# Hybrid GLA/SSD block on one core: the clamped difference of the SSD decay matrix on ScalarE instead of VectorE

## The chip, the cores and the metric

The kernel runs on one core of a Trainium2 chip. The metric is the device time of one execution in microseconds (us), lower is better; the median of three executions of the kernel before is 1922.84 us (1921.1 to 1924.56).

A core has five engines that run their own instruction streams in order: TensorE (PE in the profile, its weight loads PEld), VectorE (DVE), ScalarE (ACT), GpSimd (POOL) and SyncE (SP, which here only issues DMAs). They meet through semaphores.

## The reference, cut to what matters

One layer over 2048 tokens of width 1024, float32: RMS norm, an input projection, gated linear attention (GLA, 4 heads), a state space part (SSD, 16 heads of width 64 in 2 groups), an output projection, and a gated embedding part. The change lies in the SSD part. For each head the reference computes, chunk by chunk,

```python
cum = jnp.cumsum(dti * a_g, axis=1)
seg = cum[:, :, None] - cum[:, None, :]
decay_ij = jnp.where(causal, jnp.exp(jnp.minimum(seg, 0.0)), 0.0)
cb = jnp.einsum('bign,bjgn->bijg', ci, bi)
y = jnp.einsum('bijgh,bjghp->bighp', cb[..., None] * decay_ij, xdt)
y = y + jnp.einsum('bign,bghpn->bighp', ci, state) * jnp.exp(cum)[..., None]
```

So for each pair of tokens i, j of a chunk the decay is exp(min(cum_i - cum_j, 0)), and it multiplies the masked product cb.

## The kernel before, in words

The kernel takes the tokens in four blocks of 512 (the loop over b). Every large product is made of float32r matmuls in three parts (high by high, high by low, low by high): `prep_w` splits each weight tile with a copy on ScalarE (L172, `whi`) and a subtraction on VectorE (L173, `wlo`), and `dense_t` and `dense_n` issue the matmuls (L203 to L205, L222 to L226, in `out_proj` L794 to L796). The smaller work of GLA and SSD is written as Python generators (`gla_steps`, `ssd_steps` and others) in a list `side`; `step()` advances each by one piece between two dense products.

The order written in the file is not the order on an engine. The framework's scheduler places the instructions on each engine when the kernel is built, by priority in program order and by when it reckons an operand is ready; so independent pieces lie interleaved in the trace. On the chip each engine then keeps to that order.

In each block `ssd_steps` runs twice, once for each group g of 8 heads. It goes over four chunks t of 128 tokens:

- `make_x(t)`: transposes, `xd` on VectorE (L534), `xe` on GpSimd (L537), its split into `xh` on ScalarE (L541) and GpSimd (L542).
- `make_m(t)`: two tiles `em` (q = 0, 1) of [128, 4 heads, 128]. Partition j holds the row cum_i of four heads, read from DRAM to all partitions (L550, issued by SP). Four VectorE instructions, one for each head, subtract cum_j and clamp at zero (L552), ScalarE takes the exponential of the whole tile (L555), VectorE multiplies by `cb` (L556). The pool has three `em` tiles, so a DMA for the next waits until TensorE has read the oldest.
- the chunk: the old state times `ctl` into `ips` (L574), `em` times `xd` into `yps` (L579), the new state (L582 to L584), then on VectorE `S` (L587), `ec` (L588), `xs` (L590, L592). Then `make_x` and `make_m` of the next chunk.

`gla_steps` runs between these pieces: products into PSUM tile `ups` (from L451 on), a scaled copy `st` of the state `gT` on ScalarE (L485), the sum on VectorE (L486, `gT`), the product with `st` on TensorE (L488) and a square on ScalarE (L489). GLA and SSD share four PSUM buffers (`pss`), so a matmul that begins a new one waits until VectorE or ScalarE has read the oldest.

The change touches L552 and L555 inside `make_m`:

Of the kernel before, what the change touches and what calls it, by code (L numbers as in the profile page):

```python
# [10 lines left out]
AF = mybir.ActivationFunctionType  # L11
ALU = mybir.AluOpType
# [23 lines left out]
def hybrid_kernel(ctx, tc, x_nat, x_t, p_t, w_t, w_n0, w_n, w_o, w_g, w_p, prm, gup, cst, out):  # L36
    nc = tc.nc
    mm = nc.tensor.matmul
    act = nc.scalar.activation
# [58 lines left out]
    for h in range(GH):  # L98
        t = state.tile([P, 256], F32, name=f"gT{h}")
# [3 lines left out]
    for g in range(2):  # L103
        t = state.tile([P, 512], F32, name=f"sS{g}")
# [3 lines left out]
    for h in range(GH):  # L108
        t = sm.tile([P, NT + 1], F32, name="gD", tag=f"gD{h}", bufs=2)
# [400 lines left out]
    def ssd_steps(g, bt, ctl, xs, cx):  # L510
        h8 = slice(8 * g, 8 * g + 8)
        S = sS[g]
        S3 = S.rearrange("p (h c) -> p h c", c=64)
        dt, cum, elast, dte, cd, ecd = (cx[n] for n in ("dt", "cum", "elast", "dte", "cd", "ecd"))
        bps = pss.tile([P, TB], F32, name="pss")
        for t in range(NT):
            nc.tensor.transpose(out=bps[:, t * P:(t + 1) * P], in_=bt[:, t, :], identity=ident)
        bn = sb.tile([P, 2, NT, P], F32R, name="bn", tag="bn", bufs=SB["bn"])
        bp3 = bps.rearrange("p (a b) -> p a b", b=P)
        nc.scalar.copy(out=bn[:, 0], in_=bp3)  # L520
        tt(out=bn[:, 1], in0=bp3, in1=bn[:, 0].bitcast(F32), op=ALU.subtract)
        cps = pss.tile([P, TB], F32, name="pss")
        for t in range(NT):
            mm(out=cps[:, t * P:(t + 1) * P], lhsT=bt[:, t, :], rhs=ctl[:, t, :], start=True, stop=True)
        cb = sb.tile([P, NT, P], F32, name="cb", tag="cb", bufs=SB["cb"])
        tt(out=cb, in0=cps.rearrange("p (a b) -> p a b", b=P),
           in1=tri.unsqueeze(1).broadcast_to([P, NT, P]), op=ALU.mult)

        def make_x(t):
            xps = pss.tile([P, TB], F32, name="pss")  # L530
            for m in range(4):
                nc.tensor.transpose(out=xps[:, m * P:(m + 1) * P], in_=xs[:, m, t * P:(t + 1) * P], identity=ident)
            xd = sb.tile([P, 8, 64], F32, name="xd", tag="xd", bufs=SB["xd"])
            tt(out=xd, in0=xps.rearrange("p (h c) -> p h c", c=64),  # L534
               in1=dt[:, t, h8].unsqueeze(2).broadcast_to([P, 8, 64]), op=ALU.mult)
            xe = sb.tile([P, 8, 64], F32, name="xe", tag="tmp", bufs=SB["tmp"])
            nc.gpsimd.tensor_tensor(out=xe, in0=xd, in1=dte[:, t, h8].unsqueeze(2).broadcast_to([P, 8, 64]),  # L537
                                    op=ALU.mult)
            xh = sb.tile([P, 2, 512], F32R, name="xh", tag="xh", bufs=SB["xh"])
            xef = xe.rearrange("p h c -> p (h c)")  # L540
            nc.scalar.copy(out=xh[:, 0, :], in_=xef)  # L541
            nc.gpsimd.tensor_tensor(out=xh[:, 1, :], in0=xef, in1=xh[:, 0, :].bitcast(F32), op=ALU.subtract)  # L542
            return xd, xh

        def make_m(t):
            ems = []
            for q in range(2):
                em = sb.tile([P, 4, P], F32, name="em", tag="em", bufs=SB["em"])
                h4 = 8 * g + 4 * q
                nc.sync.dma_start(out=em, in_=cd[t, h4:h4 + 4, :].partition_broadcast(P))  # L550
                for hh in range(4):
                    nc.vector.tensor_scalar(out=em[:, hh, :], in0=em[:, hh, :],  # L552
                                            scalar1=cum[:, t, h4 + hh:h4 + hh + 1], scalar2=0.0,
                                            op0=ALU.subtract, op1=ALU.min)
                act(out=em, in_=em, func=AF.Exp)  # L555
                tt(out=em, in0=em, in1=cb[:, t, :].unsqueeze(1).broadcast_to([P, 4, P]), op=ALU.mult)  # L556
                ems.append(em)
            ec = sb.tile([P, 4, P], F32, name="ec", tag="ec", bufs=SB["ec"])
            for hf in range(2):
                src = ecd[t].rearrange("(m two) i -> two m i", two=2)[hf, 4 * g:4 * g + 4, :]  # L560
                nc.sync.dma_start(out=ec[64 * hf:64 * hf + 64], in_=src.partition_broadcast(64))
            return ems, ec

        yield
        nx = make_x(0)
        nm = make_m(0)
        yield
        for t in range(NT):
            ts = slice(t * P, (t + 1) * P)
            xd, xh = nx  # L570
            ems, ec = nm
            ips = pss.tile([P, TB], F32, name="pss")
            for m in range(4):
                mm(out=ips[:, m * P:(m + 1) * P], lhsT=S[:, m * P:(m + 1) * P], rhs=ctl[:, t, :],  # L574
                   start=True, stop=True)
            yps = pss.tile([P, TB], F32, name="pss")
            for m in range(4):
                for z in range(2):
                    mm(out=yps[64 * z:64 * z + 64, m * P:(m + 1) * P], lhsT=xd[:, 2 * m + z, :],  # L579
                       rhs=ems[m // 2][:, 2 * (m % 2) + z, :], start=True, stop=True)  # L580
            nps = pss.tile([P, TB], F32, name="pss")
            mm(out=nps, lhsT=bn[:, 0, t, :], rhs=xh[:, 0, :], start=True, stop=False)  # L582
            mm(out=nps, lhsT=bn[:, 0, t, :], rhs=xh[:, 1, :], start=False, stop=False)
            mm(out=nps, lhsT=bn[:, 1, t, :], rhs=xh[:, 0, :], start=False, stop=True)  # L584
            nc.gpsimd.tensor_tensor(out=S3, in0=S3, in1=elast[:, t, h8].unsqueeze(2).broadcast_to([P, 8, 64]),
                                    op=ALU.mult)
            tt(out=S, in0=S, in1=nps, op=ALU.add)  # L587
            tt(out=ec, in0=ec, in1=ips.rearrange("p (m i) -> p m i", i=P), op=ALU.mult)  # L588
            for m in range(4):
                stt(out=xs[:, m, ts], in0=xs[:, m, ts], scalar=pr[:, C_D + 4 * g + m:C_D + 4 * g + m + 1],  # L590
                    in1=yps[:, m * P:(m + 1) * P], op0=ALU.mult, op1=ALU.add)
            tt(out=xs[:, :, ts], in0=xs[:, :, ts], in1=ec, op=ALU.add)  # L592
            if t + 1 < NT:
                nx = make_x(t + 1)
                nm = make_m(t + 1)
                yield
# [74 lines left out]
    for b in range(NB):  # L671
# [135 lines left out]
        for t in range(NT):  # L807
            r = 1.0 if b else rn[:, t:t + 1]
            nc.vector.tensor_scalar_mul(out=lrn[:, t, :, 0:16],
                                        in0=outs[t][:, 256:272].unsqueeze(1).broadcast_to([P, 4, 16]), scalar1=r)  # L810
            stt(out=dtr[:, t, :], in0=outs[t][:, 272:288], scalar=r, in1=pr[:, C_DTB:C_DTB + 16],
                op0=ALU.mult, op1=ALU.add)
# [237 lines left out]
```

## Time and profile before

| | before |
|---|---|
| median of three executions | 1922.84 us |
| span of the profiled execution (first to last instruction) | 1915.8 us |
| TensorE busy | 1848.5 us, 96% |
| VectorE busy | 1402.0 us, 73% |
| ScalarE busy | 929.5 us, 49% |
| GpSimd busy | 372.3 us, 19% |
| DMA, mean | 108 GB/s |

The page gives the span as the profiled execution's own time; the medians are taken around the whole execution, and lie 7.0 us above it. TensorE is busy nearly throughout, so the time can fall only where TensorE stands idle or runs at a lower granted clock. Those places are found by stretches of time, not by the shares of the whole span.

### The profile page before, as it was taken

The numbers are of one execution on the slowest core, as the hardware profiler recorded it, in microseconds if no ns is written. First come the engines' busy times: TensorE is split into PE (matmuls) and PEld (weight loads), VectorE is DVE, ScalarE is ACT, GpSimd is POOL, SyncE is SP. The second block draws the span as 40 slices with busy tenths as digits, with TensorE's granted clock in tenths as the row PEclk, the third lists the DMA queues.
The fourth block names the chain that finished last, engine by engine and source line by source line (L and its number), as shares of the span: only waits on it lengthen the run. The fifth ranks groups of instructions, "written<-read, shape, count | busy, mean of one in ns | idle before, by whom it ended". The sixth has DMA issues, their size and how long they took to land.

```text
span 1915.8 us, 27885 instructions
## 1 busy us (share of the span) xinstructions
PE 1848.5 (96%) x10418; PEld 1577.9 (82%) x10418; DVE 1402.0 (73%) x2689; ACT 929.5 (49%) x1692; POOL 372.3 (19%) x331
## 2 busy tenths in 40 slices
PE   8989999999999999999999999999999999999997
PEld 7868888877887888877788788897778788889886
DVE  8996686587788668558678766855877877684676
ACT  6545443465554553346555355334655445533563
POOL 3022031043112103004311210300430211030122
PEclk9999999999999999999999999999999999999998
DMA  4332242233443233223344323322334432232232
GB/s 138 121 110 88 79 158 73 88 110 122 170 125 100 82 107 125 77 78 110 124 177 121 101 77 115 117 89 77 123 113 165 135 97 78 92 104 82 68 119 77
DMA packets 80888, 206.56 MB, mean 108 GB/s; under 512 B 8048, under 2 KB 26736, under 8 KB 80368
## 3 DMA queue, kind: packets, MB, share of 16 engines
q1 hardware_dynamic: 78768, 198.21, 32.5%
q0 software_dynamic: 1984, 6.55, 0.9%
q8 instruction: 82, 1.34, 0.3%
q14 instruction: 54, 0.44, 0.1%
HBM read 196.09 MB, written 8.65 MB: 107 GB/s over the span
## 4 chain that ended last, share of the span: by engine, by line
PE 70%; DVE 18%; ACT 5%; issue 3%; DMA 3%; POOL 1%; SPq 0%; DVEq 0%; ACTq 0%; POOLq 0%
PE psd L204 10%; PE psd L203 10%; PE psd L205 10%; PE psd L224 5%; PE psd L226 5%; PE psd L222 5%; PE psd L796 5%; PE psd L795 5%; PE psd L794 5%; DVE em L552 3%; DVE wlo L173 3%; PE pss L488 1%; DMA xp<-x_t 1%; DMA em<-cd 1%; DVE em L556 1%
## 5 line engine op out<-in xcount | busy, mean ns | idle before, releaser
L173 DVE TENSOR_TENSOR wlo<-wraw,whi 128x512 fp32r<-128x512 f32 (+1 forms) x560 | 423.9, 761 | 218.7 <-ACT whi L172 217.3
L172 ACT CAST whi<-wraw 128x512 fp32r<-128x512 f32 (+1 forms) x560 | 343.9, 620 | 466.0 <-PE psd L204 238.2
L205 PE MATMUL psd<-u,wlo 128*128 128x512 f32 x896 | 352.7, 394 | 2.1 <-DVE wlo L173 2.1
L203 PE MATMUL psd<-u,whi 128*128 128x512 f32 x896 | 353.7, 395 | 0.0
L204 PE MATMUL psd<-u,whi 128*128 128x512 f32 x896 | 351.8, 393 | 0.9 <-POOL u L331 0.9
L222 PE MATMUL psd<-whi,u 128*128 128x256 f32 (+1 forms) x960 | 276.5, 288 | 0.0
L224 PE MATMUL psd<-wlo,u 128*128 128x256 f32 (+1 forms) x960 | 273.1, 284 | 2.1 <-DVE wlo L173 2.1
L226 PE MATMUL psd<-whi,u 128*128 128x256 f32 (+1 forms) x960 | 272.6, 284 | 0.0
L300 POOL TENSOR_TENSOR sq<-sq,sqt 128x512 f32<-128x512 f32 (+1 forms) x85 | 109.9, 1293 | 610.1 <-ACT sqt L297 610.1
L794 PE MATMUL psd<-mq,whi 128*128 128x512 f32 x512 | 205.4, 402 | 0.0
L796 PE MATMUL psd<-mq,wlo 128*128 128x512 f32 x512 | 202.1, 395 | 0.0
L795 PE MATMUL psd<-mq,whi 128*128 128x512 f32 x512 | 201.0, 393 | 0.0
L205 PEld LDWEIGHTS psd<-u,wlo 128*128 128x128 f32 x896 | 168.5, 188 | 39.4 <-DVE wlo L173 3.9
L204 PEld LDWEIGHTS psd<-u,whi 128*128 128x128 f32 x896 | 168.6, 188 | 34.1 <-POOL u L331 1.2
L203 PEld LDWEIGHTS psd<-u,whi 128*128 128x128 f32 x896 | 168.6, 188 | 33.5 <-ACT whi L172 0.6
L224 PEld LDWEIGHTS psd<-wlo,u 128*128 128x128 f32 x960 | 183.6, 191 | 5.3 <-DVE wlo L173 2.9
L222 PEld LDWEIGHTS psd<-whi,u 128*128 128x128 f32 x960 | 183.6, 191 | 2.4 <-ACT whi L172 1.0
L226 PEld LDWEIGHTS psd<-whi,u 128*128 128x128 f32 x960 | 183.6, 191 | 0.0
L797 DVE TENSOR_TENSOR ht<-ht,psd 128x512 f32<-128x512 f32 x128 | 86.9, 682 | 66.2 <-PE psd L796 65.9
L796 PEld LDWEIGHTS psd<-mq,wlo 128*128 128x128 f32 x512 | 96.3, 188 | 20.6 <-issue 0.7
L203 PE MATMUL psd<-mq,whi 128*128 128x512 f32 (+1 forms) x288 | 107.3, 373 | 5.8 <-ACT pp L941 5.8
L795 PEld LDWEIGHTS psd<-mq,whi 128*128 128x128 f32 x512 | 96.4, 188 | 20.0 <-DVE mq L505 1.1
(248 smaller groups left out, 3274.0 us busy)
## 6 DMA issues: line engine op xcount, KB each, us to landing
wraw<-w_t SPq DMA_DIRECT2D x112, 512.0 KB, 3.5
wraw<-w_o SPq DMA_DIRECT2D x64, 512.0 KB, 3.5
wraw<-w_n SPq DMA_DIRECT2D x56, 512.0 KB, 3.5
em<-cd SPq DMA_DIRECT2D x64, 256.0 KB, 3.9
wraw<-w_g SPq DMA_DIRECT2D x32, 512.0 KB, 3.6
ec<-ecd SPq DMA_DIRECT2D x64, 128.0 KB, 3.0
xn<-x_nat SPq DMA_DIRECT2D x24, 256.0 KB, 3.4
xp<-x_t SPq DMA_DIRECT2D x24, 256.0 KB, 3.8
```

The lines of the kernel that those rows point to most:

```text
L172: nc.scalar.copy(out=hi, in_=s)
L173: tt(out=lo, in0=s, in1=hi.bitcast(F32), op=ALU.subtract)
L203: mm(out=ps, lhsT=hi[:, sl], rhs=rhi(k), start=(k == 0), stop=False)
L204: mm(out=ps, lhsT=hi[:, sl], rhs=rlo(k), start=False, stop=False)
L205: mm(out=ps, lhsT=lo[:, sl], rhs=rhi(k), start=False, stop=(k == KT - 1))
L222: mm(out=outs[t], lhsT=ug(0, k)[:, ts], rhs=hi[:, sl], start=first, stop=False, skip_group_check=True)
L224: mm(out=outs[t], lhsT=ug(0, k)[:, ts], rhs=lo[:, sl], start=False, stop=False, skip_group_check=True)
L226: mm(out=outs[t], lhsT=ug(1, k)[:, ts], rhs=hi[:, sl], start=False, stop=last, skip_group_check=True)
L300: self.eng.tensor_tensor(out=self.acc[:, cs], in0=self.acc[:, cs], in1=sq, op=ALU.add)
L794: mm(out=ps, lhsT=hi[:, sl], rhs=mq[:, 0, k, :], start=(k == 0), stop=False)
L795: mm(out=ps, lhsT=hi[:, sl], rhs=mq[:, 1, k, :], start=False, stop=False)
L796: mm(out=ps, lhsT=lo[:, sl], rhs=mq[:, 0, k, :], start=False, stop=(k == 3))
```

## The change

Four VectorE instructions `min(em - cum, 0)` become four ScalarE instructions `Relu(-em + cum)`, with `cum` as a bias per partition. Their result has the opposite sign, and the exponential gets the scale -1. The data, tiles, DMAs and matmuls are the same.

```diff
                 for hh in range(4):
-                    nc.vector.tensor_scalar(out=em[:, hh, :], in0=em[:, hh, :],
-                                            scalar1=cum[:, t, h4 + hh:h4 + hh + 1], scalar2=0.0,
-                                            op0=ALU.subtract, op1=ALU.min)
-                act(out=em, in_=em, func=AF.Exp)
+                    act(out=em[:, hh, :], in_=em[:, hh, :], func=AF.Relu, scale=-1.0,
+                        bias=cum[:, t, h4 + hh:h4 + hh + 1])
+                act(out=em, in_=em, func=AF.Exp, scale=-1.0)
                 tt(out=em, in0=em, in1=cb[:, t, :].unsqueeze(1).broadcast_to([P, 4, P]), op=ALU.mult)
```

## Rows read from the trace of the kernel before

**Rows 1.** The page's first part: busy time, share of the span, instructions.
```profile
PE 1848.5 (96%) x10418; PEld 1577.9 (82%) x10418; DVE 1402.0 (73%) x2689; ACT 929.5 (49%) x1692; POOL 372.3 (19%) x331
```

**Rows 2.** Windows: stretches with SSD work; length, busy time by engine, clock, DMA.
```profile
60.00:130.00 70.00, 63.73 (x368) 51.62 (x368) 65.56 (x138) 34.99 (x68) 17.14 (x15) 1.00 0.37 111
520.00:610.00 90.00, 85.62 (x507) 71.48 (x506) 77.72 (x178) 42.25 (x81) 16.71 (x15) 0.98 0.40 129
1000.00:1085.00 85.00, 80.60 (x470) 66.83 (x469) 71.53 (x161) 38.34 (x74) 16.72 (x15) 0.96 0.40 113
1480.00:1555.00 75.00, 70.70 (x403) 57.53 (x402) 66.96 (x150) 31.51 (x63) 16.93 (x15) 0.98 0.40 119
...
700.00:780.00 80.00, 76.04 (x482) 66.26 (x481) 66.80 (x131) 35.12 (x72) 19.39 (x21) 0.98 0.39 126
...
sum 610.00, PE 581.13 PEld 491.84 DVE 528.26 ACT 273.62 POOL 143.19; mean PE 72.64 PEld 61.48 DVE 66.03 ACT 34.20 POOL 17.90
```

**Rows 3.** Waits of TensorE: us in total, times, longest us.
```profile
PE pss L451 <- DVE gT L486: 15.4, 8, 2.1
PE pss L459 <- DVE ec L588: 5.5, 5, 1.6
PE pss L451 <- DVE ec L588: 2.2, 2, 2.0
```

**Rows 4.** The chain that ended last, 580 to 597: start us, us, what.
```profile
580.48 3.40 DVE em L552 x4
583.88 0.34 DVE gT L486
584.27 0.39 PE pss L451
...
594.06 2.61 DVE em L552 x4
596.67 0.34 DVE gT L486
```

**Rows 5.** Timeline of GpSimd beside the first four of those.
```profile
579.96 1.42 POOL L537 TENSOR_TENSOR xe<-xd,dte 128x512 f32<-128x512 f32 x1 [3.46 <-DVE xd L534]
581.34 1.04 POOL L585 TENSOR_TENSOR sS<-sS,elast 128x512 f32<-128x512 f32 x1
```

**Rows 6.** Line L552: min/median/max ns, and what VectorE waited for before it.
```profile
L552 DVE TENSOR_SCALAR em<-em,cum x256: 264/279/1528, 88.4 to 1713.0; 128x128 f32<-128x128 f32 x128
...
  DMA em<-cd: 5.5, 8
```

**Rows 7.** Windows just behind the first of those waits (columns as in rows 2).
```profile
585.00:590.00 5.00, 5.00 (x21) 3.31 (x21) 2.50 (x7) 1.81 (x5) 0.00 (x0) 0.66 0.14 41
```

**Rows 8.** Groups by line and shape: busy us, mean ns | idle before, releaser.
```profile
L552 DVE TENSOR_SCALAR em<-em,cum 128x128 f32<-128x128 f32 x256 | 106.7, 475 | 5.7 <-DMA em<-cd 5.5
...
L555 ACT ACTIVATE em<-em 128x512 f32<-128x512 f32 x64 | 40.4, 631 | 60.6 <-DVE em L552 60.5
L485 ACT ACTIVATE st<-gT,fs 128x256 f32<-128x256 f32 x64 | 31.9, 505 | 10.8 <-DVE gT L486 10.6
L425 ACT ACT_TABLE_LOAD x8 | 10.3, 1283 | 0.1
L950 ACT ACTIVATE gth<-gth 128x256 f32<-128x256 f32 x8 | 3.3, 418 | 7.0 <-DVE gth L949 7.0
L377 ACT ACTIVATE wk<-wk 128x64 f32<-128x64 f32 x4 | 1.0, 247 | 0.0
```

**Rows 9.** Timeline of ScalarE: two independent instructions, one behind the other.
```profile
542.06 0.62 ACT L446 ACTIVATE qm<-bc 128x512 f32<-128x512 f32 x1
542.58 0.62 ACT L447 ACTIVATE km<-bc 128x512 f32<-128x512 f32 x1
```

**Rows 10.** Timeline of VectorE, then of TensorE: a decay tile done, and its first use.
```profile
584.58 0.69 DVE L556 TENSOR_TENSOR em<-em,cb 128x512 f32<-128x512 f32 x1
...
585.51 0.43 PE L579 MATMUL pss<-em,xd 128*64 128x128 f32 x2
```

**Rows 11.** Waits of ScalarE: us in total, times, longest us.
```profile
ACT xh L541 <- POOL xe L537: 96.0, 32, 6.2
```

## The prediction, made before the changed kernel was run

> **What bounds the kernel now.** I read the page's busy shares first: TensorE is at 96% of the span [rows 1], so whatever the change does for VectorE, it pays only where TensorE stands still or is slowed. Next I cut the span into stretches around the eight places where the SSD chunks run (four blocks, two groups each) and read them as windows [rows 2]. Together they last 610.0 us, and TensorE is busy for 581.1 of them: 28.9 us idle, of the 67.3 us (1915.8 - 1848.5) that it idles in the whole span. The four stretches of group 0 hold 6.3, 4.4, 4.4 and 4.3 us of it, together 19.4; group 1 the other 9.5. VectorE is busy 528.3 us of the 610.0 there, 87%, against 73% overall; ScalarE only 273.6, 45%. So locally VectorE is the crowded engine, beside a TensorE with few holes.
>
> What ends the holes is seen in the list of waits [rows 3]: 15.4 us are waits of a GLA product (L451) for the sum `gT` on VectorE, eight times nearly 2 us, which is twice in each block; 7.7 us are waits for `ec` (L588), also VectorE. Why VectorE is late there is seen in the chain that ended last [rows 4]: in front of each late `gT` stand exactly four of the subtractions that the change takes away, 3.40 us in one place and 2.61 us in the other. These four should take 4 x 0.279 = 1.1 us by the median of the line, but its slowest took 1.528 us [rows 6], and they are slow while GpSimd works on `xe` and `sS` [rows 5]. Over the kernel the 256 subtractions cost VectorE 106.7 us, 475 ns in the mean [rows 8], so about a third of that is time lost beside GpSimd.
>
> The windows show one more loss: right behind a hole the granted clock of TensorE falls, to a mean of 0.66 over 5 us [rows 7], that is, part of that time at 1.2 instead of 2.4 GHz. From the stretches whose clock is under 1.00 [rows 2]: 90 x 0.02 + 85 x 0.04 + 75 x 0.02 + 80 x 0.02 = 8.3 us. All that there is to win in the eight stretches is then 28.9 + 8.3 = 37.2 us, 1.9%.
>
> **The change part by part.** *Removed:* 256 VectorE instructions, 106.7 us busy [rows 8]. Most of it is covered by TensorE and is worth nothing; what counts is the part in front of TensorE's holes. (a) The `gT` waits, 15.4 us: the four subtractions in front last longer (3.40 and 2.61) than the holes (about 1.9), so `gT` itself is no longer late. Next late is the decay tile, which was finished at 585.27 for a product at 585.51 [rows 10]. I count three quarters, 11.6 us (bounds 0 and 15.4). (b) The other idle time of these stretches, 28.9 - 15.4 = 13.5 us, mostly behind `ec`, which stands in VectorE's queue behind the same subtractions but also behind work that stays: half, 6.7 us (bounds 0 and 13.5). (c) The clock: it fell behind the holes, and I take half of the 8.3 back, 4.2 us (bounds 0 and 8.3). Sum of the gains 22.5 us.
>
> *Added:* 256 ScalarE instructions of 128x128 with a bias per partition. The trace has no such instruction. Nearest are one of 128x64 without a pointer operand, 247 ns, below, and one of 128x256 with a pointer operand, 505 ns, above; a 128x256 without the pointer takes 418 ns [rows 8]. The pointer thus costs 87 ns; the width costs (418 - 247) / 192 = 0.89 ns an element, so 128 elements come to 304 and with the pointer to 391 ns. I take 391 (bounds 247 and 505). Two independent instructions follow at 0.52 us though each lasts 0.62 [rows 9], so four occupy 4 x 0.391 - 3 x 0.10 = 1.26 us, and 64 tiles 81 us. Against that, ScalarE stops standing idle for the subtractions, 60.5 us [rows 8]. Its load rises from 929.5 to about 1010 us, 53%, and in the eight stretches from 45 to 58%: no bound by throughput.
>
> What can hurt is order. (d) Where GpSimd does not disturb, four subtractions take at most 1.1 us and the four Relu 1.26 to 1.56: a tile is ready about 0.35 us later (bounds 0.15 and 0.5). That matters only where TensorE waits for the tile; the pair in [rows 10] has 0.24 us to spare. How many are as tight no row here counts; I let one tile in five be: 64 / 5 x 0.35 = 4.5 us (bounds 0 and 64 x 0.5 = 32). (e) The wait for the DMA of `em`, 5.5 us in eight places [rows 6], moves from VectorE to ScalarE. Behind it now stand the copies of the weight split, `xh` and the GLA scaling, and TensorE waits for all of them in the end. Half, 2.7 us (bounds 0 and 5.5). The exponential with a scale of -1, the product with `cb`, the DMAs and SP's queue have the same instructions as before; I cost them at nothing.
>
> Total: 22.5 - 4.5 - 2.7 = 15.3 us off the profiled execution's 1915.8. That execution's span lies 7.0 us under the median of the runs, and nothing here touches the difference, so the forecast is 1922.8 - 15.3 = 1907.5, rounded to **1908 us**. What I can't read from any row is the order in which the scheduler will now place the instructions: its cover is the spread between stretches of the same code, 6.3 against 4.3 us idle in group 0 [rows 2], so some 2 us for each of eight, 16 in all, half of it to either side.
>
> One rule of the Trainium skill speaks against the change (ScalarE: Activation LUTs, section Rules for kernel authors): for `relu`, `min` and sums use VectorE, not ScalarE, as it is faster per element. The rows agree for an undisturbed instruction, 279 ns against my estimate of 391, and disagree for the mean as it runs here, 475 ns. By the rule alone the change would lose the 0.35 us of (d) on all 64 tiles and win nothing; the rival with a late decay tile, below, is where this would show.
>
> **The rivals.**
>
> *The decay tile takes over (no change).* TensorE no longer waits for `gT`, but at the same places for `em`, because DMA, Relu, exponential and product follow one another. For it: 0.24 us to spare [rows 10]. Against it: in that very place the subtractions took 3.40 us, and on ScalarE should take 1.3 to 1.6. Then (a) and (c) are gone and (b) pays for (d) and (e): 1922.8 - 6.7 + 4.5 + 2.7 = 1923.3; 1919 to 1926.
>
> *ScalarE's order becomes the bound (slower).* In every one of 32 chunks ScalarE stands waiting for GpSimd's `xe` before it makes `xh`, 96.0 us in all, 3.0 each [rows 11]; today VectorE does the subtractions meanwhile. If the Relu of both tiles are queued behind `xh`, a second tile that now is finished at 585.27 would be ready only after the wait (GpSimd's `xe` ends at 581.4 [rows 5]), `xh` and then 1.26 + 0.53 + 1.26 + 0.63 + 0.69, at 586.3: about 1 us later in each chunk, 32 us, against the gain of 22.5. That gives 1922.8 + 32 - 22.5 = 1932. It decides from 22.5 / 32 = 0.7 us per chunk on. Against it: the scheduler has ScalarE's holes of 2 to 3 us to place them elsewhere.
>
> *Everything is won.* No new wait appears: 1922.8 - 37.2 = 1886; 1886 to 1897.
>
> *Relu needs a function table of its own.* No Relu is in the trace. A load takes 1283 ns [rows 8], and two for each tile would make 128 x 1.283 = 164 us more on ScalarE, and in the eight stretches 273.6 + 81 + 164 = 519 of 610 us, 85%; VectorE's crowding would have moved over. Each tile would also be later by 2.6 us; if half of the 64 tiles made TensorE wait for 1 us of that, it gives 1922.8 + 32 = 1955. By the Trainium skill (ScalarE: Activation LUTs, section on table sets) `relu` is in every set, which would mean no load at all; no row here shows it.
>
> **How the numbers follow.** The forecast has 0.57 (its own range 1898 to 1917), everything won 0.13, the tile taking over 0.14, ScalarE's order 0.13, table loads 0.03. About 0.2% (3.8 us) is what a measurement of this kernel can tell from no change. Faster is then 0.57 + 0.13 = 0.70, within it 0.14, slower 0.13 + 0.03 = 0.16. The range goes from 1893, which leaves out about half of the case in which everything is won, to 1929, which leaves out the slower half of the two slow cases.
>
> **What would show it.** Right: no L552 on VectorE and its busy time near 1402 - 107 = 1295 us; Relu near 391 ns whether GpSimd works or not; the 15.4 us of L451 behind `gT` under 5; no clock of 0.66 near 585. Wrong: TensorE's waits for `em` at L579, now too small to be listed, of 10 us or more; ScalarE waiting for the DMA of `em` while weight copies queue; table loads on the lines of the Relu or the exponential; or a `gT` wait that stays because something else stands in front of it.

## The result, and the profile after

The changed kernel takes 1897.49 us (median; 1895.7 to 1899.03) against 1923.38 us of the kernel before beside it (1921.1 to 1924.56). The ratio is 0.9863, 95% interval 0.9845 to 0.9881: 1.4% faster, where 1908 us was forecast, in a range from 1893 to 1929.

The page's first part of the changed kernel, to be read beside [rows 1]:

```profile
PE 1843.1 (97%) x10418; PEld 1576.3 (83%) x10418; DVE 1337.3 (70%) x2433; ACT 999.2 (53%) x1948; POOL 376.2 (20%) x331
```

VectorE has its 256 instructions less, but only 64.7 us less busy time, not 106.7. ScalarE has 69.7 us more. TensorE is busy for 5.4 us less, with the same instructions, and idles 54.2 us (1897.3 - 1843.1) instead of 67.3.

Windows of the changed kernel over the stretches of [rows 2] (length, busy time by engine, clock, DMA):

```profile
60.00:130.00 70.00, 66.18 (x372) 53.91 (x371) 57.39 (x113) 45.34 (x104) 18.84 (x15) 0.98 0.39 117
520.00:610.00 90.00, 88.47 (x529) 74.74 (x528) 70.88 (x140) 57.63 (x132) 19.24 (x16) 1.00 0.44 131
...
sum 610.00, PE 597.69 PEld 506.24 DVE 477.73 ACT 341.95 POOL 153.24; mean PE 74.71 PEld 63.28 DVE 59.72 ACT 42.74 POOL 19.16
```

TensorE's idle time there is 12.3 us where it was 28.9; the comparison is rough, since all work now comes up to 18 us earlier and the stretches no longer hold quite the same (over the whole span TensorE idles 13.1 us less). VectorE is at 78% instead of 87. Waits of TensorE in the changed kernel, beside [rows 3]:

```profile
PE psd L203 <- ACT pp L940: 7.4, 3, 4.0
...
PE pss L451 <- DVE gT L486: 4.3, 4, 1.4
...
PE pss L500 <- DVE sg L494: 2.1, 3, 1.2
PE pss L459 <- DVE ec L587: 1.9, 4, 0.5
...
PE pss L451 <- DVE ec L587: 1.6, 1, 1.6
```

The `gT` waits went from 15.4 to 4.3 us, those for `ec` from 7.7 to 3.5. What is left of the `gT` waits is seen in the chain that ended last and, beside it, in the timelines of VectorE and GpSimd, at the place that answers to [rows 4] and [rows 5]:

```profile
586.19 1.47 DVE em L555 x2
587.66 1.37 issue
589.03 0.42 DVE gT L486
...
589.49 0.39 PE pss L451
```
```profile
586.11 3.00 DVE L555 TENSOR_TENSOR em<-em,cb 128x512 f32<-128x512 f32 x2
```
```profile
585.67 1.42 POOL L537 TENSOR_TENSOR xe<-xd,dte 128x512 f32<-128x512 f32 x1 [2.96 <-DVE xd L534]
587.51 1.04 POOL L584 TENSOR_TENSOR sS<-sS,elast 128x512 f32<-128x512 f32 x1 [0.42 <-PE pss L573]
588.52 1.72 POOL L542 TENSOR_TENSOR xh<-xe,xh 128x512 fp32r<-128x512 f32 x1
```

Now the two products with `cb` (L555, L556 before) stand in front of `gT`, and they are long while GpSimd works: 3.00 us for two (what the chain calls issue is the end of the second), where one takes 0.69 us by the median. The groups by line say the same of the whole (busy us, mean ns | idle before): first the product in the kernel before, then product and Relu in the changed one. Behind them the view of line L552 gives the Relu's min/median/max and what ScalarE waited for before it.

```profile
L556 DVE TENSOR_TENSOR em<-em,cb 128x512 f32<-128x512 f32 x64 | 46.6, 747 | 0.3
```
```profile
L555 DVE TENSOR_TENSOR em<-em,cb 128x512 f32<-128x512 f32 x64 | 60.6, 969 | 17.7 <-ACT em L554 17.3
```
```profile
L552 ACT ACTIVATE em<-em,cum 128x128 f32<-128x128 f32 x256 | 83.7, 391 | 59.2 <-DMA em<-cd 44.4 <-DVE xs L589 3.6 <-PE pss L488 3.5
```
```profile
L552 ACT ACTIVATE em<-em,cum x256: 384/388/406, 88.7 to 1692.0; 128x128 f32<-128x128 f32 x128
...
  DMA em<-cd: 44.4, 20
```

The Relu lasts 384 to 406 ns wherever it stands, while the subtraction it replaces went from 264 to 1528 [rows 6]. The product with `cb` rose from 747 to 969 ns in the mean: part of VectorE's time beside GpSimd was not removed, it moved to the next instruction. And ScalarE now waits 44.4 us for the DMAs of `em`.

### The profile page after: what moved, and what is told of

It is laid out like the page before. It is cut to its first block, busy times and chain, and to the rows that moved or that the text cites. A ratio compares the mean times of both kernels' runs of the same rounds, so it can differ in the third digit from the quotient of the medians.

```text
span 1897.3 us, 27870 instructions
## 1 busy us (share of the span) xinstructions
PE 1843.1 (97%) x10418; PEld 1576.3 (83%) x10418; DVE 1337.3 (70%) x2433; ACT 999.2 (53%) x1948; POOL 376.2 (20%) x331
## 4 chain that ended last, share of the span: by engine, by line
PE 74%; DVE 13%; ACT 6%; issue 4%; DMA 2%; POOL 1%; SPq 0%; DVEq 0%; ACTq 0%; POOLq 0%
PE psd L205 11%; PE psd L204 11%; PE psd L203 11%; PE psd L224 5%; PE psd L226 5%; PE psd L222 5%; PE psd L795 5%; PE psd L794 5%; PE psd L793 5%; DVE wlo L173 3%; PE pss L488 1%; DMA xp<-x_t 1%; PE pss L451 1%; PE pss L578 1%; PE pss L573 1%
## 5 line engine op out<-in xcount | busy, mean ns | idle before, releaser
L173 DVE TENSOR_TENSOR wlo<-wraw,whi 128x512 fp32r<-128x512 f32 (+1 forms) x560 | 438.4, 787 | 237.3 <-ACT whi L172 235.8
L552 ACT ACTIVATE em<-em,cum 128x128 f32<-128x128 f32 x256 | 83.7, 391 | 59.2 <-DMA em<-cd 44.4
```

The lines of the kernel that those rows point to most:

```text
L173: tt(out=lo, in0=s, in1=hi.bitcast(F32), op=ALU.subtract)
```

## The experiments

The theory to test: the gain comes from VectorE's queue, where the subtractions stood in front of `gT` and `ec` in the SSD stretches. Rivals: the scheduler rebuilt the order of everything and the gain is a lucky order; or the decay tile's own chain got shorter. A second question came out of the rows above: is it the four instructions as such, or GpSimd beside them?

**One group alone.** First group 0 only (the diff, against the kernel before; the other branch has its lines), then group 1 only (`g == 1`).

```diff
+                if g == 0:
+                    for hh in range(4):
+                        act(out=em[:, hh, :], in_=em[:, hh, :], func=AF.Relu, scale=-1.0,
+                            bias=cum[:, t, h4 + hh:h4 + hh + 1])
+                    act(out=em, in_=em, func=AF.Exp, scale=-1.0)
+                else:
...
```

> Only the tiles of group 0 have the clamped difference on ScalarE; group 1 keeps the four VectorE subtractions. Queue theory (the time comes from TensorE's waits behind the subtractions in VectorE's queue in the SSD stretches; group 0 held 19.4 of the 28.9 us idle and 6.7 of the 8.3 us of low clock): 16 to 20 us faster than the kernel before, gT waits of L451 down to about 4 us as with both groups. Rival, the rebuilt order of instructions (any edit here lets the scheduler place everything anew, and the gain is that): no relation to the groups, anything from 0 to 26 us faster.

> The other half alone: group 1 on ScalarE, group 0 as before. Queue theory: 5 to 9 us faster than the kernel before, and the gT waits of L451 stay near 15 us, since they lie in group 0; with the run of group 0 alone the two gains sum to 26 us within 4. Rival, rebuilt order: the two don't sum, and the gT waits fall here too.

Measured: group 0 alone 1903.44 us against 1923.23, ratio 0.9905 (0.9873 to 0.9936), group 1 alone 1914.81, ratio 0.9965 (0.9946 to 0.9984). By the ratios that is 18.3 and 6.7 us, together 25.0; by the medians 19.8 and 8.4, together 28.2. Either way both lie in the bands of the queue theory, and the sum is that of the whole change (25.9) within the 4 us allowed. With group 0 alone TensorE waits little for `gT` at L451 (the first line; another 4.9 us of such waits stand at L585). With group 1 alone the wait of [rows 3] is still there whole (the second):

```profile
PE pss L451 <- DVE gT L486: 0.9, 2, 0.6
```
```profile
PE pss L451 <- DVE gT L486: 15.6, 8, 2.2
```

A lucky order would have had no reason to follow the groups.

**The subtractions back as idle work.** The changed kernel, with four subtractions per tile that nobody reads.

```diff
                 act(out=em, in_=em, func=AF.Exp, scale=-1.0)
+                scr = sb.tile([P, P], BF16, name="scr", tag="scr", bufs=1)
+                for hh in range(4):
+                    nc.vector.tensor_scalar(out=scr, in0=xf[:, hh * P:(hh + 1) * P],
+                                            scalar1=cum[:, t, h4 + hh:h4 + hh + 1], scalar2=0.0,
+                                            op0=ALU.subtract, op1=ALU.min)
```

Here `xf` is `xd` of the same chunk; to make room for `scr`, the convolution weights are scaled where they stand instead of in a copy.

> The changed kernel, and beside it four VectorE subtractions of 128x128 for each tile, with the same operands' form, from xd into a scratch tile that nobody reads (bf16, for want of room), emitted where the old ones stood. The decay tile does not depend on them. Queue theory: VectorE's queue is as full as before, so most of the gain goes: 1912 to 1924 us, gT waits of L451 back over 10 us. Rival (the decay tile's own chain became shorter or surer on ScalarE, the queue does not matter): 1896 to 1902 us.

Measured: 1931.33 us, ratio 1.0049 (1.0029 to 1.0068). All of the gain went and more, so the band of 1912 to 1924 was missed on the slow side, and the rival's 1896 to 1902 is out. Its waits of TensorE, then its group of idle subtractions:

```profile
PE pss L583 <- DVE em L560: 10.7, 9, 1.6
PE pss L451 <- DVE ec L592: 10.1, 6, 2.2
PE pss L451 <- DVE gT L486: 8.6, 5, 2.1
```
```profile
L557 DVE TENSOR_SCALAR scr<-xd,cum 128x128 bf16<-128x128 f32 x256 | 127.4, 498 | 2.9
```

The waits for `gT` came back to 8.6 us, not over 10 as expected; the rest shows as waits for `ec` and for the decay tile's product, all behind the same queue. So the gain needs VectorE's queue to be relieved. A small gain from the tile's own chain could still be hidden here, since these subtractions keep VectorE busy for longer (127.4 us) than the old ones did (106.7).

**The subtractions left out.** The kernel before without L552; nothing is added to ScalarE. (The clamp and the difference are missing from what it computes.)

```diff
-                for hh in range(4):
-                    nc.vector.tensor_scalar(out=em[:, hh, :], ...)
                 act(out=em, in_=em, func=AF.Exp)
```

> The kernel before with the four subtractions left out (the exponential takes the DMA's tile as it is), so VectorE is relieved and ScalarE gets nothing. Queue theory with the forecast's terms: gains of 22.5 us without the 7.2 us that the Relu cost, so 4 to 8 us faster than the changed kernel: 1890 to 1894 us. If ScalarE's added work is fully hidden: 1896 to 1899 us, the same as the changed kernel. If the rebuilt order is what counts: anywhere, slower than the changed kernel too.

Measured: 1900.15 us, ratio 0.9892 (0.9854 to 0.9931). That is not faster than the changed kernel (0.9845 to 0.9881; the intervals overlap), and it lies 1 us above the band for hidden work, too. So the 7.2 us that terms (d) and (e) put on the Relu are not there: ScalarE's 69.7 us are covered. The late `gT` of L451 is gone from TensorE's waits; what is left of it stands at L575. ScalarE waits for the DMAs of `em` in this run as well, since the exponential now reads their tile first, so the run can't say what those waits cost. One line of TensorE's waits, one of ScalarE's:

```profile
PE pss L575 <- DVE gT L486: 1.0, 4, 0.2
```
```profile
ACT em L551 <- DMA em<-cd: 18.3, 19, 3.2
```

**GpSimd beside VectorE.** Two of GpSimd's three operations of a chunk are left out (`xe`'s product and the decay of `S`), in the kernel before and in the changed one.

```diff
-            nc.gpsimd.tensor_tensor(out=xe, in0=xd, in1=dte[...], op=ALU.mult)
-            xef = xe.rearrange("p h c -> p (h c)")
+            xef = xd.rearrange("p h c -> p (h c)")
...
-            nc.gpsimd.tensor_tensor(out=S3, in0=S3, in1=elast[...], op=ALU.mult)
```

> The kernel before with two of GpSimd's three operations of each chunk left out (xe's product with dte, so xh is made of xd itself, and the decay of the state S). Contention theory (the subtractions are long in front of gT because GpSimd works beside them): L552 falls from 475 ns to about 350, the gT waits from 15.4 us to under 8, the time to 1903 to 1914 us. Rival, mere occupation (four more instructions in the queue, GpSimd or not): gT waits over 12 us and 1917 to 1924 us, less the little that a shorter chain to xh gives.

> The changed kernel with the same two GpSimd operations left out. Contention theory: the gap between this pair (this run against the one before it) shrinks from 26 us to 12 or less, since there is less left to be blocked; the product with cb falls from 969 ns to about 800. Rival, mere occupation: the gap stays at 20 us or more.

Measured: before without them 1885.95 us, ratio 0.9814 (0.98 to 0.9829); changed without them 1883.51, 0.9796 (0.9779 to 0.9812). The gap of 25.9 us has shrunk to 2.4, and with these intervals can't be told from nothing. The time of the first is far below the band of 1903 to 1914: GpSimd cost the kernel before more than I had thought. Group of the subtractions and wait for `gT` in the kernel before so cut:

```profile
L549 DVE TENSOR_SCALAR em<-em,cum 128x128 f32<-128x128 f32 x256 | 81.8, 378 | 10.6 <-DMA em<-cd 10.5
```
```profile
PE pss L451 <- DVE gT L486: 2.3, 7, 0.4
```

All 256 subtractions are still in VectorE's queue, and TensorE waits 2.3 us in place of 15.4. In front of each of these seven `gT` stand four subtractions, as before, but they take 1.9 us there and not 2.61 to 3.40. The number of instructions alone was not the trouble. In the changed kernel so cut the product with `cb` takes 747 ns in the mean, where about 800 was expected.

**The two operations moved instead of left out.** The same arithmetic, on VectorE: first `xe` alone (the first two lines of the diff), then `xe` and the decay of `S`, each in both kernels.

```diff
-            nc.gpsimd.tensor_tensor(out=xe, in0=xd, in1=dte[...], op=ALU.mult)
+            tt(out=xe, in0=xd, in1=dte[...], op=ALU.mult)
...
-            nc.gpsimd.tensor_tensor(out=S3, in0=S3, in1=elast[...], op=ALU.mult)
+            tt(out=S3, in0=S3, in1=elast[...], op=ALU.mult)
```

> The same move of xe in the kernel before. Contention theory: L552 falls from 475 to about 380 ns, which wins back the 22 us of xe on VectorE: 1915 to 1924 us. Occupation: 22 us more in the crowded queue and no relief, 1928 to 1940 us.

> The changed kernel with xe's product with dte on VectorE (32 instructions of about 0.68 us, 22 us busy) instead of GpSimd (1.42 us each). If contention is the larger matter in VectorE's queue: the product with cb falls from 969 ns to about 800 and xh comes 0.7 us earlier, 1888 to 1896 us, faster than the changed kernel. If occupation is: VectorE gets 22 us back into the crowded stretches, 1900 to 1908 us.

> The same two moves in the kernel before. Contention theory: though VectorE gets 44 us more, 1890 to 1900 us, and the gap to the changed kernel with the same moves falls under 12 us. Occupation: 1905 us or more, and a gap of 18 us or more.

> The changed kernel with both xe's product and the decay of S on VectorE; GpSimd keeps only xh's low part in a chunk. Contention theory: 1882 to 1887 us, near the 1883.5 us of the kernel in which both were left out, since VectorE now has room. Occupation: each of the two costs VectorE 22 us, 1890 us or more.

Measured, with `xe` moved: before 1904.61 us (ratio 0.9911, 0.9896 to 0.9926), changed 1885.41 (0.9811, 0.9797 to 0.9826). With both moved: before 1889.81 (0.9841, 0.9825 to 0.9856), changed 1883.16 (0.9807, 0.979 to 0.9825). VectorE got 32 and 64 instructions more, of 0.68 to 0.74 us in the mean, and both kernels became faster. With `xe` moved both came out below either theory's band; with both moved the kernel before lies just under the contention band and the changed one in it, and the gap of 6.6 us is under the 12. The groups and waits of the kernel before with `xe` moved, and then with both:

```profile
L552 DVE TENSOR_SCALAR em<-em,cum 128x128 f32<-128x128 f32 x256 | 97.3, 434 | 4.1 <-DMA em<-cd 4.0
```
```profile
PE pss L451 <- DVE gT L486: 6.7, 7, 1.3
```
```profile
L552 DVE TENSOR_SCALAR em<-em,cum 128x128 f32<-128x128 f32 x256 | 85.4, 406 | 2.3 <-DMA em<-cd 2.3
```
```profile
PE pss L451 <- DVE gT L486: 2.9, 4, 1.3
```

The mean of L552 falls from 475 over 434 to 406 ns as GpSimd is relieved, and the wait for `gT` from 15.4 over 6.7 to 2.9 us. The changed kernel with both moved has the lowest median of those that compute the whole, though its interval overlaps that of `xe` moved alone: its page has TensorE at 98%.

```profile
PE 1836.7 (98%) x10418; PEld 1573.6 (84%) x10418; DVE 1357.2 (72%) x2497; ACT 997.7 (53%) x1948; POOL 293.1 (16%) x267
```

**Contention or a shorter chain?** To move `xe` also makes `xh` come earlier (0.68 us instead of 1.42 and a hop less). So `xe` stays on VectorE, and GpSimd does the same product again, for nobody.

```diff
             tt(out=xe, in0=xd, in1=dte[...], op=ALU.mult)
+            xu = sb.tile([P, 8, 64], F32, name="xu", tag="tmp", bufs=SB["tmp"])
+            nc.gpsimd.tensor_tensor(out=xu, in0=xd, in1=dte[...], op=ALU.mult)
```

> The kernel before with xe on VectorE, and GpSimd still doing the same product into a tile that nobody reads. The chain to xh is as short as with xe moved (1904.6 us), GpSimd's claim on VectorE is back. Contention theory: L552 back from 434 to about 475 ns and 1918 to 1935 us (VectorE also has xe now). Rival, the shorter chain to xh made the gain of the move: 1902 to 1908 us.

> The same on the changed kernel (xe on VectorE, GpSimd doing the product for nobody). Contention theory: the product with cb back from 751 to about 900 ns, 1893 to 1903 us instead of 1885.4. Rival, the shorter chain: 1884 to 1888 us.

Measured: before 1925.66 us (ratio 1.0018, 1.0002 to 1.0035), changed 1907.71 (0.9933, 0.9918 to 0.9949). Against `xe` moved without it, the useless product costs 21.1 and 22.3 us and takes back the whole gain of the move, and more; the shorter chain gives nothing that is seen. The first time lies in the contention band, the second some 5 us above it. Groups of the first and its wait for `gT`, then groups of the second:

```profile
L555 DVE TENSOR_SCALAR em<-em,cum 128x128 f32<-128x128 f32 x256 | 105.1, 471 | 1.1 <-DMA em<-cd 1.1
...
L537 DVE TENSOR_TENSOR xe<-xd,dte 128x512 f32<-128x512 f32 x32 | 35.9, 1123 | 0.0
```
```profile
PE pss L451 <- DVE gT L486: 13.5, 7, 2.1
```
```profile
L558 DVE TENSOR_TENSOR em<-em,cb 128x512 f32<-128x512 f32 x64 | 60.1, 967 | 13.0 <-ACT em L557 12.4
L537 DVE TENSOR_TENSOR xe<-xd,dte 128x512 f32<-128x512 f32 x32 | 40.2, 1256 | 0.0
```

L552 (L555 here) is back at 471 ns, the wait for `gT` at 13.5 us, the product with `cb` at 967 ns, and VectorE's own `xe`, 680 ns without the useless product, takes 1123 and 1256. A caveat: the useless product also holds one of the four temporary tiles, which may cost some of its own.

All pairs together, medians in us. The rows come from three groups of runs; the kernel before, measured beside each, took 1923.4, 1922.2 and 1921.5 us, so 1 to 2 us between rows mean nothing:

| GpSimd's work in a chunk | subtractions on VectorE | Relu on ScalarE | gap |
|---|---|---|---|
| `xe`, decay of `S`, low part of `xh` (as given) | 1923.4 | 1897.5 | 25.9 |
| the same, but `xe` is for nobody | 1925.7 | 1907.7 | 18.0 |
| decay of `S`, low part of `xh` | 1904.6 | 1885.4 | 19.2 |
| low part of `xh` (two moved) | 1889.8 | 1883.2 | 6.6 |
| low part of `xh` (two left out) | 1886.0 | 1883.5 | 2.4 |

So the change is worth 26 us while GpSimd has three operations of a chunk, and a tenth to a quarter of that when it has only the low part of `xh` to make. The useless product shows that GpSimd's work beside VectorE makes VectorE's instructions long and brings the waits of TensorE back. It does not show that this makes the gap: the product costs either form about 20 us, and the gap is 18.0 us with it and 19.2 without. The gap closes mainly when the decay of `S` goes. Whether that is because the decay lay beside the subtractions, as in [rows 5], or because the state's own chain became shorter, was not tried with a useless decay.

## Why the prediction was right, and where its steps were not

*What bounds the kernel:* right. The time came out of TensorE's holes in the SSD stretches, group 0 two to three times as much as group 1 (18.3 and 6.7 us by the ratios, 19.8 and 8.4 by the medians; the idle time had it as 19.4 to 9.5).

*Term (a), the `gT` waits:* 11.1 us gone (15.4 - 4.3), 11.6 forecast. But the next late instruction was not the decay tile as I had it; it was the product with `cb`, long beside GpSimd in VectorE's queue just as the subtractions had been. The term left 3.8 us standing for one reason, and 4.3 stayed for another: that the sizes agree is luck.

*Terms (b), (d) and (e):* together +2.0 us in the trace (13.1 us less idle, of it 11.1 behind `gT`), against 6.7 - 4.5 - 2.7 = -0.5. The `ec` waits fell by 4.2, and small new waits came (`sg` 2.1, `pp` from 5.8 to 7.4). (d), the later tile, cost nothing that is seen: the list of TensorE's waits has none for `em` at L578. (e) was mis-sized: ScalarE waits 44.4 us for DMAs, not 5.5. I had read the wait off VectorE, which in the kernel before came to most tiles after the DMA had landed: it waited at 8 of 64 [rows 6]. What the longer wait costs was not measured apart from the rest. Much of it is waiting under another name, since ScalarE now waits 42.4 us for `xe`, where it waited 96.0 [rows 11]:

```profile
ACT xh L541 <- POOL xe L537: 42.4, 22, 5.6
```

*Term (c), the clock:* TensorE's busy time fell by 5.4 us, 4.2 forecast. The slow stretch of [rows 7] is gone, and one has come in the first block, again behind a hole: in the 5 us before it TensorE was busy for 2.70 (windows of the changed kernel, columns as above):

```profile
110.00:115.00 5.00, 5.00 (x28) 4.04 (x27) 3.07 (x7) 3.88 (x12) 3.03 (x3) 0.66 0.45 151
...
585.00:590.00 5.00, 4.04 (x27) 3.38 (x25) 5.00 (x6) 4.54 (x14) 3.91 (x3) 1.00 0.42 145
```

*The base:* this step failed. In the trace the gain is 18.5 us (1915.8 to 1897.3), near the 15.3 forecast; by the medians it is 25.9. I took the 7.0 us between span and median to lie outside the span. Every execution whose span is on record with its time (110 of them) is 1.7 to 2.1 us longer than its span, 1.8 as a rule. By that rule the profiled execution of the kernel before, whose own time is not on record, was one of about 1917.6 us, 5.8 under the median beside it, and that of the changed kernel, 1899.03 us, was 1.5 over its own: 18.5 + 5.8 + 1.5 = 25.8.

*VectorE's busy time:* forecast 1295, measured 1337 us. I saw that a third of the subtractions' time was lost beside GpSimd and took it as removed with them. A part of it shows up again in other instructions of the queue: the product with `cb` is busy 14.0 us more, the weight split L173 14.5 us more (762 to 788 ns in the mean for its 128x512 form).

*The Relu:* 391 ns estimated, 391 measured; no table loads on its lines. *The rule against the change*, for `relu` use VectorE (the Trainium skill, ScalarE: Activation LUTs, section Rules for kernel authors), did not decide: the figure behind it there is for bf16, and these tiles are float32. The rows still agree for an undisturbed instruction, 279 against 388 ns by the medians, and disagree for the mean, 475 against 391. The Trainium skill also has the rule that speaks for the change (SBUF — State Buffer, section Who interferes with whom): VectorE and GpSimd share a pair of ports, and where both need it, the instruction that issues first holds it for its whole length and the other is blocked; ScalarE has its own. The runs agree: 264 to 1528 ns on VectorE beside GpSimd, 384 to 406 on ScalarE.

*The rivals:* the tile taking over and ScalarE's order did not come, nor table loads. Everything won, 1886, was not reached either; it took the move of GpSimd's work to get to 1883. But the time, 1897.49, lies between the ranges of the two: half a microsecond under the forecast's own (1898 to 1917) and as much above that of everything won (1886 to 1897). By the trace's gain of 18.5 us it would have been 1904.3, within the forecast's own; the rest is the base.

## What to carry to other kernels

When a short VectorE instruction has a mean far above its median, look at what GpSimd does at that moment: here moving two GpSimd operations per chunk onto the engine that looked crowded won some 30 us of 1923, about as much as taking 107 us of work off it (ratios 0.9841 and 0.9863; the intervals overlap). To find where such time counts, cut the span into stretches and read what stands in the queue in front of the instruction that TensorE waits for. And put a forecast on the time of the execution that was profiled, not on the median, until the difference between the two is known.

## What the runs showed of the hardware that was not expected

Executions of one kernel spread by the clock that TensorE was granted: twenty executions of the kernel before, beside the first four experiments, took 1915.01 us (mean clock 0.994) to 1931.46 us (0.989), while the four of the changed kernel took 1895.7 to 1899.03 (0.997 to 0.995). The order is not strict: at a mean clock of 0.992 the kernel before took 1917.11 to 1924.43 us. Which comes first, the lower clock or the longer holes, these runs do not say.

Not every VectorE instruction is lengthened beside GpSimd. In the kernel before, `ec` (L588), which reads one operand from PSUM, took 670 to 686 ns in all 32 places, though 11 of them overlap a GpSimd instruction; the product with `cb` (L556), with both operands in SBUF and the same size, went from 671 to 1532.
